# A decoder trunk in fp32: split weights held as three pieces of 2048 columns in place of five of 1024

## The chip, the cores and the metric

The kernel runs on one core of a Trainium2 chip. TensorE multiplies matrices, loading a stationary operand of 128x128 and streaming the other through it; VectorE, ScalarE and GpSimd do the elementwise work; SyncE issues the transfers from the chip's memory (HBM) into the on-chip memory of 128 partitions. The metric is the device time of one execution in microseconds (us), the median of three runs.

## The reference

Two layers on 256 tokens of 1024 channels, all in float32:

```python
a    = rmsnorm(h)
proj = a @ w_in[i]                       # q, k, v, u, c, b: 512 columns each
attn = stick_breaking_attention(qnorm(q), knorm(k), v)      # 8 heads of 64
conv = b * causal_depthwise_conv(c * u)                     # 3 taps
h   += concat(rmsnorm(attn), rmsnorm(conv)) @ w_o[i]
f    = rmsnorm(h)
h   += swiglu(f)                         # layer 0: dense, hidden width 3584
h   += moe_swiglu(f)                     # layer 1: the best 2 of 8 experts of the same width
h   += sigmoid(rmsnorm(h) @ w_g[i]) * (p[i] @ w_p[i])       # the embedding
```

with `swiglu(x) = (silu(x @ w1) * (x @ w3)) @ w2`.

## The kernel before

**Numbers in two parts.** Each fp32 operand is held as a rounded high part and the low remainder, and each product is made of three matmuls: input low by weight high (line 181), input high by weight low (182), high by high (183). So the low part of a weight is wanted one matmul after its high part.

**Weights.** A weight comes in halves of 128 partitions by 2048 columns, 1 MB each. `load` (line 85) gets a slot of the pool `rawp` and issues the transfer. `split` makes the two parts, in slots of the pool `wp`: `wh` by a copy on ScalarE (L94, called a cast below) and `wl` by a subtraction on VectorE (L95). `plan` lists the halves in the order of use, and `parts` cuts each into pieces of `PART` columns, which are the unit of splitting. `loads(upto)` issues transfers up to a part, `prepare(upto)` splits up to a part, and `weights()` hands out the next half and prepares parts so that `ahead[0]` are held, the one in use among them:

```python
NPART = 5        # split parts held
rawp = pool("rawp", 14)
wp = pool("wp", NPART)
prepare(max(i0 + m, i0 + ahead[0] - keep))
```

With `once=True` (in the experts) it also prepares one more part as soon as the second part of a half is taken. A slot of `wp` is free again when the last matmul that reads it is done; a slot of `rawp` when both the cast and the subtraction have read it. The pool `rawp` serves other things too: parts of gathered tokens, `y`, `hout`, the embedding `pp`, q and k.

`pieces[0]` is 2 up to the experts: there each part is split by two casts and two subtractions of half its columns. From the experts on it is 1.

**The order of work.** TensorE's order is the program's throughout. From the routing on, ScalarE's and VectorE's order is the program's too; before that a scheduler places their instructions. So in the experts a cast that waits for a slot of `wp` holds up everything behind it on ScalarE, and a subtraction that waits for its cast everything behind it on VectorE.

**Experts.** `Moe.route` chooses each token's experts and gathers the first two experts' tokens. `Moe.main` goes through eight experts of seven blocks (512 of the 3584 hidden columns). A block has four up halves (12 matmuls of 512 columns each, into `pe`), with the activation `s` on ScalarE (L843) behind the second and the product `m` on VectorE (L846) behind the fourth; then two down halves of the block before (12 matmuls each, into `y`), and between them the four transposes of `m` (L581, `pt`), whose result is again split, `th` on ScalarE (L585) and `tl` on VectorE (L586). After an expert's last down half its `y` is split (L872 and L873), and in the second block of the next expert it is brought back to the tokens' order and added to `hout` (L880 to L882). Within every second expert but the last the next pair's tokens are gathered (L804, `pg`; split at L210 and L211).

**Embedding.** Its two tensors, `p` (512 columns) and `w` (2048 columns), are handed out by two calls of `weights()` at once; 24 matmuls go to `ppp`, and ScalarE copies each result to `pp` (L1048). In layer 1 this goes along with the third block of the last expert, behind its second down half (line 982); in layer 0 it stands ahead of the last block's down halves in the dense feed-forward.

**End.** The last expert's second down half, the return to the tokens' order, and four gate matrices' halves (`gated_embedding`), from where the output is written.

Of the kernel before, what the change touches and what calls it, by code (L numbers as in the profile page):

```python
# [9 lines left out]
F32R = mybir.dt.float32r  # L10
# [6 lines left out]
P = 128  # L17
D = 1024
S = 256
NT = S // P  # L20
KD = D // P
NE = 8
# [3 lines left out]
PART = 1024      # columns of a weight part, split at a time  # L26
NPART = 5        # split parts held
LOADS = (9, 14)  # weight halves whose loads go ahead of the experts, before and after h is split
EMB = 2          # block of the last expert that the last embedding goes along with
EPS = 1e-6  # L30

# columns of the parameter pack
# [6 lines left out]
# columns of the constant pack  # L39
# [5 lines left out]
def trunk(ctx: ExitStack, tc: tile.TileContext, a, out):  # L45
# [4 lines left out]
    rawp = pool("rawp", 14)  # L50
# [8 lines left out]
    # ---- parameters and constants  # L59
# [5 lines left out]
    lt = cst[:, C_LT:C_LT + P]        # [k, m] = k < m  # L65
    iota = cst[:, C_IOTA:C_IOTA + P]
    elow = cst[:, C_E:C_E + 64].rearrange("p (e f) -> p e f", f=NE)   # [e, f] = f < e
    mhalf = const.tile([P, 8], F32, name="mhalf")
    nc.vector.memset(mhalf, -0.5)
    gtr = const.tile([P, P], F32R, name="gtr")     # [k, m] = k > m  # L70
# [9 lines left out]
    # ---- building blocks  # L80
# [17 lines left out]
    def emb(l):  # L98
        """p and w of the embedding, for weights()"""
        return [(a["pT"][l].rearrange("p k s -> p (k s)"), S), (a["w_p"][l], D)]  # L100

    # the weights in the order of their use, in parts of PART columns, split ahead of it
    plan = []
# [29 lines left out]
    def loads(upto):  # L133
        """parts up to that one, loaded"""
        for i in range(len(ready), min(upto, len(parts))):
            (src, n), c = parts[i]
            if i not in raws:
                w = src.shape[-1]
                raw = load(src, w, 2 if i < 4 else 1)
                for j in range(-(-w // PART)):  # L140
                    raws[i + j] = raw[:, j * PART:min(w, (j + 1) * PART)]

    def prepare(upto, eng=nc.vector):
        """parts up to that one, split"""
        loads(upto)
        while len(ready) < min(upto, len(parts)):
            i = len(ready)
            n = parts[i][0][1]
            raw = raws.pop(i)
            ready.append([x.rearrange("p (k n) -> p k n", n=n) for x in split(raw, raw.shape[-1], pieces[0], eng)])  # L150

    def weights(src=None, n=None, once=False, keep=0):
        """function of k that gives block k of the next of the plan, or, where src is given, of that;
        once: each k is used once, in order; keep: parts before it that are still in use"""
        if src is not None:
            width = src.shape[-1]
            raw = load(src, width)
            pw = min(width, PART)
            p = [[x.rearrange("p (k n) -> p k n", n=n) for x in split(raw[:, c:c + pw], pw)]
                 for c in range(0, width, pw)]  # L160
        else:
            (src, n), _ = parts[used[0]]
            i0, m = used[0], -(-src.shape[-1] // PART)
            used[0] += m
            prepare(max(i0 + m, i0 + ahead[0] - keep))
            p = ready[i0:i0 + m]
            ready[i0:i0 + m] = [None] * m
        kp = p[0][0].shape[1]
        seen = set()

        def at(k):
            c = k // kp
            if once and c not in seen:
                seen.add(c)
                if c:
                    prepare(i0 + c + ahead[0])
            return [x[:, k % kp, :] for x in p[c]]
        return at
# [11 lines left out]
    class TokenRstd:  # L190
        """1 / rms of each token of h, [P, NT]: part(n) for each half of the channels, then done()"""
# [21 lines left out]
    def x_tiles(raw=False):  # L213
        """two parts of a transposed input; of two that live at a time, one is raw: in weights' slots"""
        return [rawp.tile([P, KD, S], F32R, tag="raw", name=n) if raw else xp.tile([P, KD, S], F32R, tag=n, name=n)
                for n in ("xh", "xl")]

    class Transposed:
        """gain * h over channels, in two parts, and the token factors; step(k) does channels k, k + 1 of 128"""
# [6 lines left out]
        def step(self, k):  # L226
            # a bank for each channel block, so that two engines read at a time
# [10 lines left out]
        def rest(self):  # L238
            self.step(4)
            self.step(6)  # L240
            if ahead[0] < NPART:
                ahead[0] = NPART
                prepare(used[0] - 2 + NPART)
            self.rs.part(0)
            self.rs.part(1)
            self.rs.done()

    def run(chunks, between=()):
        """chunks in order; between: {i: closures run after chunk i}"""
# [6 lines left out]
    def gemm_tokens(xh, xl, k0s, pss, done, srcs=None, first=False, final=False):  # L256
        """chunks of pss[t] = sum over the next halves [P, 4 k, 512] of x(tokens t).T @ w, from the k's in k0s on;
        first: both token blocks of the first half go along with its k's; final: the last token block goes in two
        parts of the columns, each with its bank and its done()"""
# [46 lines left out]
    # ---- the mixer: attention and short convolution  # L306
    def mixer(l, xt, after):
        """xt: transposed input, whose steps 4 and 6 are still to do where l > 0; after: makes the next one"""
        with tc.tile_pool(name="att", bufs=2) as ap, tc.tile_pool(name="att1", bufs=1) as a1:
            if l == 0:  # L310
# [5 lines left out]
                ready.extend([wp.tile([P, 2, 512], F32R, tag=n, name=n) for n in ("wh", "wl")] for _ in range(2))  # L316
# [5 lines left out]
                for k in range(KD):  # L322
                    scaled_split(xh[:, k, :], xl[:, k, :], xr[:, k, :], par[:, G_MIX + k:G_MIX + k + 1])
                    if k < 4:
                        wh, wl = [x[:, k % 2, :] for x in ready[k // 2]]
# [13 lines left out]
            def v_g():  # L339
                """the values over tokens, and the convolution's input"""  # L340
# [5 lines left out]
            # q, k normalised, of each (j, t)  # L346
            qn = rawp.tile([P, 2 * NT, 512], F32, tag="raw", name="qn")

            def tokens_in():
                # the squares summed over the channels, to tokens  # L350
# [7 lines left out]
            def consts():  # L358
                # of 0 and 1, so the rounding keeps them
# [9 lines left out]
            # q, k: normalised per head over tokens, then transposed; v stays over tokens  # L369
# [31 lines left out]
            # token factors over the free axis, on every partition  # L401
# [136 lines left out]
            # output projection: the two normalised parts, each with its token factor  # L538
# [38 lines left out]
    # ---- feed-forward, dense  # L577
# [11 lines left out]
    def dense(l, xt, fill, nxt):  # L589
        """fill: closures of work for the wait before the last block; nxt(): makes the next transposed input"""  # L590
# [69 lines left out]
    # ---- feed-forward, routed  # L660
    class Parts:
        """h over tokens, in two parts; part(n, t): half n of the channels of token block t"""
# [15 lines left out]
        def block(self, k, t):  # L678
            """channel block k of token block t: low, high"""
            return [self.x[k // 4][:, i, t, k % 4 * P:(k % 4 + 1) * P] for i in (1, 0)]  # L680

    class Route:
        """the two parts of h, and from its logits each expert's tokens and gates"""
# [17 lines left out]
        def half(self, n, t):  # L701
            """channels of half n of token block t, transposed"""
# [17 lines left out]
        def choose(self, mp, rp):  # L720
            self.mp, self.rp = mp, rp
            # rank of each logit; the lower index goes first where two are equal
# [20 lines left out]
            # slot of each token in its expert, and the tokens of each expert  # L743
# [11 lines left out]
        def counts(self):  # L755
            """the largest number of tokens of an expert"""
# [5 lines left out]
        def gates(self):  # L762
            """softmax over the selected logits"""
# [17 lines left out]
    class Gather:  # L781
        """one-hot token to slot matrices of the experts es, and their tokens over channels, in two parts"""
# [10 lines left out]
        def step(self, k, pl=tp, tag="t", apart=False):  # L793
            """channel blocks k, k + 1; apart: each in a bank of its own"""
# [18 lines left out]
        def slots(self, i):  # L813
            """slot to token matrix of expert i, and the token factor of each slot"""
# [12 lines left out]
    def expert_up(ws, b, g, i, rk, fp):  # L827
        """chunks of hidden block b of the slots i of g; rk(): the token factor of each slot"""
# [46 lines left out]
    def combine(hin, hout, y, slT, gcol, n, pl=tp, tag="t", late=None):  # L875
        """hout = hin + gate * (slots back to tokens), half n of the channels; late: takes the sums, to be done then"""
# [12 lines left out]
    class Moe:  # L889
# [7 lines left out]
        def route(self):  # L897
            """choice of the experts, and the first two's tokens"""
# [5 lines left out]
            prepare(n + 1)  # L904
# [6 lines left out]
            loads(n + 2 * LOADS[1])  # L911
# [5 lines left out]
            prepare(n + 2)  # L917
# [5 lines left out]
        def main(self, first, fill):  # L923
            """every expert's first 128 tokens; first: the first two experts' Gather;
            fill: closures of work to do along with the last expert"""
# [57 lines left out]
            # the last block  # L983
# [22 lines left out]
        def over(self):  # L1006
            """every expert's tokens from the 129th on"""
# [24 lines left out]
    # ---- per-layer embedding  # L1032
    def embedding(srcs=None):
        """four closures that make p @ w, of srcs or the next of the plan, and a function that gives
        the tile it goes to"""
# [16 lines left out]
    def gated_embedding(l, pp, xt, p2, nxt=None, src=None):  # L1052
        """h + sigmoid(x @ w) * pp: into h, or, of the last layer, out; nxt(): makes the next transposed input"""
# [29 lines left out]
    with tc.manual_schedule(engines={mybir.EngineType.PE}):  # L1083
# [8 lines left out]
        with tc.tile_pool(name="moe1", bufs=1) as m1, tc.tile_pool(name="moe2", bufs=2) as mp:  # L1092
# [11 lines left out]
            with tc.manual_schedule(engines={mybir.EngineType.Activation, mybir.EngineType.DVE}):  # L1104
                loads(len(ready) + 2 * LOADS[0])
# [4 lines left out]
            # an expert has more than 128 tokens: the others are added, and the end is done again  # L1110
# [9 lines left out]
def _layout(inp):  # L1120
# [4 lines left out]
    def rows(w, kb, nb):  # L1125
        """[..., kb*128*?, N] -> [..., N/nb blocks, K/(kb*128) parts, 128, kb*nb]"""
# [72 lines left out]
```

## Time and profile before

| | |
|---|---|
| median of three runs (1543.73, 1543.99, 1545.69) | 1543.99 us |
| the profiled execution: span from first to last instruction | 1541.0 us |
| TensorE (PE) busy, share of the span, instructions | 1521.9 us, 99%, 7249 |
| TensorE's weight loads (PEld) | 1261.5 us, 82%, 7249 |
| VectorE (DVE) | 1282.6 us, 83%, 1553 |
| ScalarE (ACT) | 1096.0 us, 71%, 1470 |
| GpSimd (POOL) | 92.7 us, 6%, 96 |
| bytes moved, mean rate | 445.84 MB, 289 GB/s |

The span leaves out what lies before the first and behind the last instruction, 3.0 us against the median. A busy engine is one with an instruction under way, waiting for nothing. TensorE's matmuls overlap each other, so that its busy share tells only that it is seldom without one, not at what pace they follow. The experts run from about 540 to 1485 us of the span.

### The profile page before, as it was taken

What the parts mean: (1) busy time and instruction counts of PE and PEld (TensorE: products, weight loads), DVE (VectorE), ACT (ScalarE), POOL (GpSimd) and SP (SyncE); (2) the same over time, 40 slices, a digit from 0 to 9 for tenths busy, and PEclk for the clock granted to TensorE, in tenths of its full rate; (3) what the DMA queues carried; (4) which work ended last, traced back from release to release, by engine and by line L of the source; (5) the groups of instructions that cost most, each with busy time, mean ns of one, the idle gap of its engine ahead of it and who ended that gap; (6) DMA issues with size and microseconds to landing.
All of it is one profiled execution on the core that took longest, in us unless ns stands there. A gap on an engine that the chain in (4) does not pass through costs nothing.

```text
span 1541.0 us, 19945 instructions
## 1 busy us (share of the span) xinstructions
PE 1521.9 (99%) x7249; PEld 1261.5 (82%) x7249; DVE 1282.6 (83%) x1553; ACT 1096.0 (71%) x1470; POOL 92.7 (6%) x96
## 2 busy tenths in 40 slices
PE   7999999999999999999999999999999999999998
PEld 6888888887888788888888888888888888888886
DVE  7886555556788799899899999999999999999895
ACT  5756444446675687878777778787787887877874
POOL 3430000000243000000000000000000000000000
PEclk9999999999999899999999999999999999999999
DMA  9656554343435699897999998999998899999960
GB/s 359 251 197 241 191 186 176 137 162 111 169 148 203 236 379 371 313 349 288 360 372 375 351 361 328 375 408 378 353 360 331 313 362 368 377 343 338 362 259 30
DMA packets 64043, 445.84 MB, mean 289 GB/s; under 512 B 7104, under 2 KB 9024, under 8 KB 10432
## 3 DMA queue, kind: packets, MB, share of 16 engines
q1 hardware_dynamic: 63936, 444.48, 75.8%
q8 instruction: 59, 0.97, 0.2%
q14 instruction: 48, 0.39, 0.1%
HBM read 443.40 MB, written 1.05 MB: 288 GB/s over the span
## 4 chain that ended last, share of the span: by engine, by line
PE 97%; DVE 1%; DMA 0%; ACT 0%; issue 0%; SPq 0%; POOL 0%; DVEq 0%; ACTq 0%
PE pe L181 13%; PE pe L183 13%; PE pe L182 13%; PE y L183 8%; PE y L182 8%; PE y L181 8%; PE p L183 3%; PE p L182 3%; PE p L181 3%; PE pt L581 2%; PE pu L181 2%; PE pu L182 1%; PE pu L183 1%; PE pj L181 1%; PE pj L183 1%; PE pj L182 1%
## 5 line engine op out<-in xcount | busy, mean ns | idle before, releaser
L95 DVE TENSOR_TENSOR wl<-raw,wh 128x1024 fp32r<-128x1024 f32 (+1 forms) x999 | 1017.6, 1058 | 178.8 <-ACT wh L94 167.3
L94 ACT CAST wh<-raw 128x1024 fp32r<-128x1024 f32 (+1 forms) x1000 | 881.4, 913 | 242.8 <-PE pe L183 78.9
L181 PE MATMUL pe<-wh,xl 128*128 128x512 f32 x896 | 350.6, 391 | 0.0
L183 PE MATMUL pe<-wh,xh 128*128 128x512 f32 x896 | 349.2, 390 | 0.0
L182 PE MATMUL pe<-wl,xh 128*128 128x512 f32 x896 | 348.6, 389 | 0.0
L181 PE MATMUL y<-wh,tl 128*128 128x512 f32 x560 | 226.2, 404 | 0.0
L182 PE MATMUL y<-wl,th 128*128 128x512 f32 x560 | 220.8, 394 | 0.5 <-DVE wl L95 0.5
L183 PE MATMUL y<-wh,th 128*128 128x512 f32 x560 | 220.9, 395 | 0.0
L183 PEld LDWEIGHTS pe<-wh,xh 128*128 128x128 f32 x896 | 168.1, 188 | 36.2
L182 PEld LDWEIGHTS pe<-wl,xh 128*128 128x128 f32 x896 | 168.3, 188 | 35.9 <-DVE wl L95 0.4
L181 PEld LDWEIGHTS pe<-wh,xl 128*128 128x128 f32 x896 | 168.2, 188 | 35.1
L183 PEld LDWEIGHTS y<-wh,th 128*128 128x128 f32 x560 | 105.1, 188 | 25.2
L182 PEld LDWEIGHTS y<-wl,th 128*128 128x128 f32 x560 | 105.3, 188 | 22.7 <-DVE wl L95 1.2
L181 PEld LDWEIGHTS y<-wh,tl 128*128 128x128 f32 x560 | 105.3, 188 | 21.6 <-ACT wh L94 0.2
L181 PE MATMUL p<-wh,xl 128*128 128x512 f32 x224 | 87.8, 392 | 0.0
L183 PE MATMUL p<-wh,xh 128*128 128x512 f32 x224 | 87.3, 390 | 0.0
L182 PE MATMUL p<-wl,xh 128*128 128x512 f32 x224 | 87.2, 389 | 0.0
L585 ACT CAST th<-pt 128x512 fp32r<-128x512 f32 x70 | 40.9, 586 | 41.7 <-PE pt L581 41.7
L95 POOL TENSOR_TENSOR wl<-raw,wh 128x1024 fp32r<-128x1024 f32 x1 | 2.4, 2372 | 990.8 <-ACT wh L94 990.8
L181 PE MATMUL pu<-xh,wl 128*128 128x256 f32 x192 | 56.4, 294 | 0.0
L182 PE MATMUL pu<-xl,wh 128*128 128x256 f32 x192 | 54.2, 282 | 0.0
L183 PE MATMUL pu<-xh,wh 128*128 128x256 f32 x192 | 54.2, 282 | 0.0
(203 smaller groups left out, 1565.4 us busy)
## 6 DMA issues: line engine op xcount, KB each, us to landing
raw<-m_w SPq DMA_DIRECT2D x336, 1024.0 KB, 5.7
raw<-d_w SPq DMA_DIRECT2D x42, 1024.0 KB, 4.8
raw<-w_in SPq DMA_DIRECT2D x22, 1024.0 KB, 6.9
raw<-w_o SPq DMA_DIRECT2D x8, 1024.0 KB, 6.7
raw<-w_g SPq DMA_DIRECT2D x8, 1024.0 KB, 4.8
raw<-w_p SPq DMA_DIRECT2D x2, 1024.0 KB, 4.8
raw<-w_in SPq DMA_DIRECT2D x4, 256.0 KB, 4.4
raw<-w_in SPq DMA_DIRECT2D x2, 512.0 KB, 8.8
```

The source lines that it names most:

```text
L94: nc.scalar.copy(wh[:, cs], raw[:, cs])
L95: eng.tensor_sub(wl[:, cs], raw[:, cs], wh[:, cs].bitcast(F32))
L181: nc.tensor.matmul(ps, ll, rh, start=start, stop=False)
L182: nc.tensor.matmul(ps, lh, rl, start=False, stop=False)
L183: nc.tensor.matmul(ps, lh, rh, start=False, stop=stop)
L581: nc.tensor.transpose(pt[:, c * P:(c + 1) * P], m[:, c * P:(c + 1) * P], ident)
L585: nc.scalar.copy(th, pv)
```

## The change

A part becomes a whole half: `PART` is 2048 and `NPART` is 3, so `wp` holds 3 x 2048 columns for each of `wh` and `wl` in place of 5 x 1024. `rawp` has 13 slots in place of 14. What counted two parts to a half now counts one: the loads ahead of the experts (9 halves, then 13 in place of 14), the split of the very first half, the two transfers that it and the second half are loaded in, and the numbers in `prepare`. In the routing one `prepare` of one part goes, and one stays. At the end `ahead[0] = 3` is no longer below `NPART`, so `Transposed.rest` prepares nothing there; the part that GpSimd subtracts is a whole half. Since `pieces[0]` is as it was, pieces are 1024 columns up to the experts (512 before) and 2048 in the experts (1024 before). The embedding's `p` has 512 columns and takes a slot of its own as before, now one of 2048. The rest of the difference is comments, left out here.

```diff
-PART = 1024      # columns of a weight part, split at a time
-NPART = 5        # split parts held
-LOADS = (9, 14)  # weight halves whose loads go ahead of the experts, before and after h is split
+PART = 2048
+NPART = 3
+LOADS = (9, 13)
...
-    rawp = pool("rawp", 14)
+    rawp = pool("rawp", 13)
...
-                raw = load(src, w, 2 if i < 4 else 1)
+                raw = load(src, w, 2 if i < 2 else 1)
...
-                prepare(used[0] - 2 + NPART)
+                prepare(used[0] - 1 + NPART)
...
-                ready.extend([wp.tile([P, 2, 512], F32R, tag=n, name=n) for n in ("wh", "wl")] for _ in range(2))
+                ready.append([wp.tile([P, 4, 512], F32R, tag=n, name=n) for n in ("wh", "wl")])
...
-                        wh, wl = [x[:, k % 2, :] for x in ready[k // 2]]
+                        wh, wl = [x[:, k, :] for x in ready[0]]
...
-            prepare(n + 1)
...
-            loads(n + 2 * LOADS[1])
+            loads(n + LOADS[1])
...
-            prepare(n + 2)
+            prepare(n + 1)
...
-                loads(len(ready) + 2 * LOADS[0])
+                loads(len(ready) + LOADS[0])
```

The order in which ScalarE works around the last expert's embedding, from the activation of the block before it; `pp` are the copies of the embedding, `th` the split of the transposed `m`. Before:

```order
L843 ACTIVATE s<-pe,rslot 128x512
L94 CAST wh<-raw 128x1024 x4
L94 CAST wh<-raw 128x512
L94 CAST wh<-raw 128x1024
L585 CAST th<-pt 128x512
L94 CAST wh<-raw 128x1024 x3
L1048 COPY pp<-ppp 128x512 x4
L94 CAST wh<-raw 128x1024 x6
```

and of the changed kernel:

```order
L843 ACTIVATE s<-pe,rslot 128x512
L94 CAST wh<-raw 128x2048 x2
L94 CAST wh<-raw 128x512
L585 CAST th<-pt 128x512
L94 CAST wh<-raw 128x2048 x2
L1047 COPY pp<-ppp 128x512 x4
L94 CAST wh<-raw 128x2048 x3
```

The cast of 512 columns is `p`. Behind it stood the first part of `w` ahead of `th`; now the whole of `w` stands behind `th`, and one whole half behind it is cast ahead of the copies.

The order in which VectorE works from the end of an expert into the second block of the next; `y` is the split of the expert's result, `hout` the sum over the experts (the last two names are the two token blocks of h). Before:

```order
L95 TENSOR_TENSOR wl<-raw,wh 128x1024 x2
L586 TENSOR_TENSOR tl<-pt,th 128x512
L95 TENSOR_TENSOR wl<-raw,wh 128x1024 x2
L873 TENSOR_TENSOR y<-y 128x512 x2
L95 TENSOR_TENSOR wl<-raw,wh 128x1024 x4
L882 SCALAR_TENSOR_TENSOR hout<-pc,gate,h_97 128x512
L882 SCALAR_TENSOR_TENSOR hout<-pc,gate,h_98 128x512
L95 TENSOR_TENSOR wl<-raw,wh 128x1024 x2
```

The same place of the changed kernel:

```order
L95 TENSOR_TENSOR wl<-raw,wh 128x2048
L586 TENSOR_TENSOR tl<-pt,th 128x512
L95 TENSOR_TENSOR wl<-raw,wh 128x2048
L873 TENSOR_TENSOR y<-y 128x512 x2
L95 TENSOR_TENSOR wl<-raw,wh 128x2048 x2
L882 SCALAR_TENSOR_TENSOR hout<-pc,gate,h_97 128x512
L882 SCALAR_TENSOR_TENSOR hout<-pc,gate,h_98 128x512
L95 TENSOR_TENSOR wl<-raw,wh 128x2048
```

The sequence is the same, with one subtraction of 2048 columns where two of 1024 stood: the two of `y` and the sums `hout` stand behind whole halves as before.

## Rows read from the trace of the kernel before

**Rows 1.** Busy time by stretch: window, length, PE, PEld, DVE, ACT, POOL, clock, DMA, GB/s.
```profile
545.00:1420.00 875.00, 875.00 (x3988) 720.33 (x3988) 813.60 (x790) 695.17 (x764) 0.00 (x0) 1.00 0.92 354
```

**Rows 2.** Waits at the tile raw, 540 to 1500 us: releaser, us, times.
```profile
  DMA raw<-m_w: 2.0, 4
```

**Rows 3.** Groups by form, whole span (columns as in the page's part 5).
```profile
L95 DVE TENSOR_TENSOR wl<-raw,wh 128x1024 fp32r<-128x1024 f32 x678 | 801.0, 1220 | 69.1 <-ACT wh L94 58.9 <-DMA raw<-m_w 1.4
L94 ACT CAST wh<-raw 128x1024 fp32r<-128x1024 f32 x679 | 700.4, 1053 | 120.8 <-PE pe L183 78.6 <-PE y L183 30.5 <-DVE wl L95 2.4
L95 DVE TENSOR_TENSOR wl<-raw,wh 128x512 fp32r<-128x512 f32 x319 | 215.9, 716 | 109.8 <-ACT wh L94 108.4
L94 ACT CAST wh<-raw 128x512 fp32r<-128x512 f32 x319 | 180.4, 618 | 121.8 <-PE p L183 59.5 <-PE y L183 42.2 <-PE po L183 9.3
```

**Rows 4.** Timeline of a regular block: start, length, engine, operation, [idle before, releaser].
```profile
802.93 0.39 PE L181 MATMUL pe<-wh,xl 128*128 128x512 f32 x1
803.13 0.69 ACT L843 ACTIVATE s<-pe,rslot 128x512 f32<-128x512 f32 x1 [0.30 <-PE pe L183]
...
803.72 3.19 ACT L94 CAST wh<-raw 128x1024 fp32r<-128x1024 f32 x3
...
804.79 4.74 DVE L95 TENSOR_TENSOR wl<-raw,wh 128x1024 fp32r<-128x1024 f32 x4 [0.70 <-ACT wh L94]
...
808.37 0.40 PE L181 MATMUL y<-wh,tl 128*128 128x512 f32 x1
...
811.18 0.60 PE L581 MATMUL pt<-cst,m 128*128 128x128 f32 x4
```

**Rows 5.** Timeline of the block after expert 0's end.
```profile
651.61 2.00 ACT L94 CAST wh<-raw 128x1024 fp32r<-128x1024 f32 x2
...
654.97 1.28 DVE L873 TENSOR_TENSOR y<-y 128x512 fp32r<-128x512 f32 x2
...
667.89 0.74 DVE L846 SCALAR_TENSOR_TENSOR m<-pe,rslot,s 128x512 f32<-128x512 f32 x1
...
669.26 0.60 PE L581 MATMUL pt<-cst,m 128*128 128x128 f32 x4
```

**Rows 6.** Timeline of the first expert's first blocks.
```profile
530.17 5.93 ACT L94 CAST wh<-raw 128x1024 fp32r<-128x1024 f32 x6
...
536.59 0.66 PE L581 MATMUL pt<-cst,m 128*128 128x128 f32 x4 [0.22 <-DVE m L846]
```

**Rows 7.** Routing: a stretch (columns of rows 1), then gathering matmuls in the chain.
```profile
516.00:518.00 2.00, 2.00 (x11) 2.00 (x11) 1.84 (x5) 0.92 (x2) 1.58 (x1) 0.50 0.00 0
...
515.44 6.63 PE pg L804 x32
...
734.40 1.91 PE pg L804 x16
```

**Rows 8.** Timeline of the last expert's embedding.
```profile
1425.76 2.00 ACT L94 CAST wh<-raw 128x1024 fp32r<-128x1024 f32 x2
...
1427.87 0.40 PE L181 MATMUL ppp<-wh,wl 128*128 128x512 f32 x1
...
1434.03 5.80 ACT L94 CAST wh<-raw 128x1024 fp32r<-128x1024 f32 x6
...
1435.11 5.76 DVE L95 TENSOR_TENSOR wl<-raw,wh 128x1024 fp32r<-128x1024 f32 x5 [4.73 <-ACT wh L94]
```

**Rows 9.** Timeline of the last down half of layer 0.
```profile
356.85 3.22 ACT L94 CAST wh<-raw 128x512 fp32r<-128x512 f32 x6
...
358.26 0.50 PE L182 MATMUL y<-wl,th 128*128 128x512 f32 x1 [0.23 <-DVE wl L95]
...
359.46 0.50 PE L182 MATMUL y<-wl,th 128*128 128x512 f32 x1 [0.25 <-DVE wl L95]
```

**Rows 10.** Timeline in the attention of layer 1.
```profile
439.89 1.42 POOL L447 TENSOR_TENSOR spl<-sp,sph 128x384 fp32r<-128x384 f32 x1 [0.72 <-ACT sph L445]
...
441.46 0.34 PE L455 MATMUL later<-spl,gtr 128*128 128x384 f32 x1
```

## Prediction

> **What bounds the kernel now.** I read the engines' shares of the page first, then the busy time by stretch, then single groups and the order of time. Across the experts TensorE is busy 875.00 of 875.00 us [rows 1]; its matmuls of 512 columns start every 0.227 us (0.234 in the down projection), and nothing releases them but the matmul before. VectorE is busy 813.60 us of the same stretch. So TensorE sets the end, VectorE is some 7% behind it, and ScalarE has room. The loads are early: in the whole stretch of the experts a cast or subtraction waited 2.0 us in all for a load, four times [rows 2]. A gain can come only from places where TensorE already waits; a loss comes wherever a split weight now arrives later than TensorE wants it.
>
> **The price of a piece.** A subtraction on 1024 columns takes 1.22 us and one on 512 takes 0.72 [rows 3]; four in a row take 4.74 us, one every 1.18 us [rows 4]. From 512 to 1024 the duration grows by 0.50 to 0.53 us, so 2048 columns should take 1.22 + 1.06 = 2.29 us and one should start every 2.25 us. The bounds are 2.05 (the fixed share grows smaller still) and 2.44 (twice 1.22, no saving). A cast takes 1.05 us on 1024 and 0.62 on 512, so 1.91 on 2048 (bounds 1.8 and 2.1). One half (2048 columns) therefore costs VectorE 2.25 us in place of 2.36, some 0.7 us less in a block of six halves. As TensorE waits for none of that, the saving itself is worth nothing.
>
> What changes is how late a weight is. Before, a buffer of 1024 columns was free after six matmuls, its cast began at once, and the subtraction followed 1.05 us later. Now the buffer is free after twelve, and the subtraction starts 1.91 us after the cast does. The slots for split weights grow from five of 1024 to three of 2048, so a half may still be split while the two before it are in use: 2 x 2.72 = 5.44 us for 0.20 + 1.91 + 0.04 + 2.29 + 0.06 = 4.50 us of work, where 0.20 is the time from the start of TensorE's next half to ScalarE's start on what that releases (802.93 to 803.13 [rows 4]), and the small numbers are the gaps between a cast, its subtraction and the matmul behind.
>
> The Trainium skill, Perfetto Trace Analysis, section Optimizing Scalar/DVE Operations, has a rule for each side: larger operations raise throughput if the engine is saturated, and where Scalar or Vector aren't saturated but cause bubbles on other engines, breaking instructions up lets work finish sooner. By the first the 0.7 us of 56 blocks would be 39 us of gain; VectorE was not what TensorE waited for, so the sum takes nothing of it. By the second the change goes the wrong way, which is what the terms below say from rows.
>
> **The regular block** (48 of 56): no loss, with little cover. The up half that starts at 802.93 releases the activation at 803.13 and after it the cast at 803.72 [rows 4]. With the new durations this cast ends at 805.63 and its subtraction at 807.96, and TensorE wants it with its second matmul at 808.37 + 0.23 = 808.60: cover 0.6 us. The next subtraction starts at 807.92 and is followed at 810.17 by the product m (0.74), done at 810.91. The transposes of m stand at 811.18: cover 0.2 us, before 1.0. The term is 0; it becomes a loss from 2.36 us a half on.
>
> **The block after an expert's end** (7 times). VectorE has two more subtractions for y and four sums hout there, and is busy without a break from 654.97 to the product m at 667.89, which ends 0.63 us ahead of the transposes at 669.26 [rows 5]. Now the y subtractions queue behind a whole half, whose cast starts where it started before, at 651.61: 651.61 + 1.91 + 0.04 + 2.25 = 655.8 in place of 654.97. Four halves behind that save some 0.1. So m is done at 669.4 and reaches TensorE 0.2 us late: 7 x 0.2 = 1.4 us, between 0 and 7 x 0.73 = 5.1 (at 2.36 us a half). In the three experts with a new pair gathered VectorE has two more subtractions of 512 in a block, 1.4 us; the fourth up half comes 0.1 late: 0.3 us.
>
> **The first expert.** The casts start only at 530.17, and TensorE already waits for m, until 536.59 [rows 6]. Now 530.17 + 1.91 + 0.04 + 2 x 2.25 + 0.74 + 0.06 = 537.4: 0.8 us later. In the routing the one split left between the choice and the gathered tokens is twice as long, 1.1 us more ahead of eight short subtractions; the gathering matmuls beside them run at a granted clock of 0.50, 1.2 GHz (32 of them in 6.63 us, later 16 in 1.91 [rows 7]), and hide most: 0.3 us. Together 1.1 (0.5 to 2).
>
> **The last expert's embedding, the largest term.** Its two tensors lie between two blocks, p (512 columns) and w (2048), and p fills a slot of 2048. Both are in use at once, so only one half is held ahead. First, w takes the slot of the down half before last. Before, its first part was cast from 1425.76 and was there for the embedding's second matmul at 1427.87 + 0.23 = 1428.10 [rows 8]. Now: 1425.76 + 1.91 + 0.04 + 2.29 + 0.06 = 1430.06, 2.0 us late. Second, behind the embedding TensorE has one half ready and starts on it 24 matmuls later, at 1433.35; the second can only be cast when the embedding's copies are done, at 1434.03. Before, its first part was subtracted from 1435.11 to 1436.33, and TensorE wanted it at 1433.35 + 2.72 + 0.23 = 1436.30. Now 1434.03 + 1.91 + 0.04 + 2.29 + 0.06 = 1438.33: 2.0 us late, 1.9 more than before. Sum 3.8 (3 to 4.5).
>
> **The same place in layer 0.** Pieces there are half a slot: 1024 columns now, 512 before. The last down half is cast from 356.85 and TensorE waits for its subtractions twice already, until 358.26 and 359.46 [rows 9], 0.75 us in all past its pace. With pieces of 1024 the first is there at 356.85 + 1.04 + 0.05 + 1.22 + 0.06 = 359.22, the second 0.5 us behind its want: the two waits grow to about 1.95, less 0.2 that the same pieces save a little later: 1.0 (0.5 to 1.5). Elsewhere in layer 0 a half lasts 5.44 us on TensorE, twice the window, and hides everything.
>
> **Attention and the first matmuls.** The scheduler puts weight pieces between the short steps of the heads. One step ends at 441.31 on GpSimd where TensorE wants it at 441.46 [rows 10]: a piece that is 0.5 us longer ahead of such a step shows. I take 0.5 us a layer, 1.0, between 0 and 4. The first matmuls of the second weight half wait for one piece of 1024 in place of 512: 0.3 (0 to 0.5).
>
> **Raw slots.** One slot less is 2.8 us less lead, and a slot is held some 0.7 us longer. The few waits for loads are small [rows 2], so nothing. The tail takes nothing either: the split given to GpSimd becomes twice as long, but is for the second half of the last gate, 7 us away.
>
> **Sum.** 0.3 + 1.0 + 1.0 + 1.1 + 1.4 + 0.3 + 3.8 = 8.9 us. The profiled span is 1541.0 us, 3.0 below the median of 1544.0, which the change doesn't touch: 1541.0 + 8.9 + 3.0 = 1552.9, say **1553 us**, 0.6% slower.
>
> **Rivals.** (a) *VectorE saves nothing on a wider piece*: a half takes twice 1.22 = 2.44 us. Then the cover of the regular block is gone by 0.17 us, 48 x 0.17 = 8; the seven blocks lose 1.1 each, 8; the rest 9: 1569. Against it: the growth from 512 to 1024 [rows 3]. Values between give 1555 to 1565. (b) *Only the forced places lose*: embedding, first expert, layer 0's end, 5.9 us: 1550. For it: the other terms are each a few tenths, within what I can read off. (c) *Not slower: the pace of the down projection.* Its matmuls start every 0.234 us, those of the up projection every 0.227 (808.37 to 811.18 holds 12 of the one, 802.93 to 808.37 holds 24 of the other [rows 4]). If VectorE's and ScalarE's many short accesses cause this 0.007, fewer of them win up to 1344 x 0.007 = 9 us and cancel the sum: 1544; with (b), 1541. It decides from 4 ns a matmul on. Against it: the up projection runs under the same traffic at the faster pace. A smaller relief of the kind: if TensorE's clock doesn't fall to 1.2 GHz in the routing, 6.63 - 2 x 1.91 = 2.8 us come back; with (b) that is 1547. (d) *The change isn't what it says*: before the experts each half is split in two pieces, so 2048 wide pieces exist only there; this is in the sum.
>
> **How the numbers follow.** Forecast 1553: 0.50. (a) or between, 1557 to 1569: 0.12. (b) 1550: 0.14. No change by (c) or by the clock: 0.16. Faster, (c) with (b): 0.08. A measurement of this kernel tells 0.2% (3 us) from no change. Slower: 0.50 + 0.12 + 0.14 = 0.76; the same 0.16; faster 0.08. The range takes in (b), part of no change, and (a) up to half of it: 1545 to 1563.
>
> **What would show it.** In the trace of the changed kernel: a subtraction on 2048 columns of 2.29 us; TensorE waiting some 2 us twice around the last embedding, for the second matmul of the embedding and of the half after the next; about 0.2 us at the transposes in one block per expert and none in the others; in the first expert 0.8; all else as before. It is wrong if TensorE shows waits in every block (then a piece is dearer), if the embedding's waits aren't there (then a slot is free earlier than I read), if the time sits in attention, or if the matmul pace moves.

## The result

The changed kernel takes 1557.49 us (median of five runs, 1556.61 to 1558.88) against 1544.54 us before: a ratio of 1.0083, 95% interval 1.0073 to 1.0094, 12.95 us slower. The forecast was 1553, with 1545 to 1563 for the range. The profiled execution spans 1556.9 us.

Groups by form of the changed kernel, which answer to [rows 3]:

```profile
L95 DVE TENSOR_TENSOR wl<-raw,wh 128x2048 fp32r<-128x2048 f32 x338 | 768.0, 2289 | 112.7 <-ACT wh L94 110.1 <-DMA raw<-m_w 1.3
L94 ACT CAST wh<-raw 128x2048 fp32r<-128x2048 f32 x339 | 647.3, 1913 | 111.4 <-PE pe L183 86.7 <-PE y L183 17.2 <-DMA raw<-m_w 7.5
...
L95 DVE TENSOR_TENSOR wl<-raw,wh 128x1024 fp32r<-128x1024 f32 x160 | 194.4, 1245 | 115.6 <-ACT wh L94 115.6
...
L94 ACT CAST wh<-raw 128x1024 fp32r<-128x1024 f32 x160 | 161.8, 1048 | 136.0 <-PE p L183 61.8 <-PE y L183 43.3 <-PE po L183 13.2
```

The price of a piece came out as forecast: 2.289 us for a subtraction on 2048 columns (2.29), 1.913 for a cast (1.91). VectorE is busy 1234.0 us in place of 1282.6, and the kernel is slower all the same.

TensorE executes the same 7249 instructions in the same order in every kernel of this study, so that the time from one fixed instruction to another can be set side by side. This table is worked out so from the starts in the traces. "Start" is from the first matmul to the 101st instruction. Counted from 0, the other stretches lie between the instructions 1600, 1760, 2000 and 2570 and between 2630, 2700, 6700 and 6800. From 100 to 1600 all twelve traces take 298.31 us, and behind 6800 they differ by less than 0.4 us. The routing (2570 to 2630) isn't listed, since the granted clock there differs between executions of one kernel: 13.9 and 12.7 us in the two traces of the kernel before, 12.5 to 14.2 in all. The lines below "changed" are the experiments of the next section.

| stretch of TensorE (us) | start | layer 0's end | gates, layer 0 | attention | first expert | experts | last embedding |
|---|---|---|---|---|---|---|---|
| before | 27.13 | 36.29 | 50.86 | 90.46 | 15.20 | 877.93 | 22.66 |
| before, a second trace | 31.35 | 36.31 | 50.85 | 90.46 | 15.21 | 877.94 | 22.64 |
| changed | 30.47 | 37.19 | 51.43 | 90.85 | 15.93 | 883.61 | 26.63 |
| old widths everywhere | 28.94 | 36.31 | 51.15 | 90.46 | 15.21 | 877.94 | 23.20 |
| 1024 in the experts | 29.58 | 37.20 | 51.41 | 90.85 | 15.20 | 877.94 | 23.22 |
| six parts of 1024 | 30.56 | 35.19 | 50.86 | 90.45 | 15.22 | 877.93 | 22.39 |
| raw slots alone | 30.95 | 36.30 | 50.87 | 90.46 | 15.22 | 877.92 | 22.63 |
| p elsewhere | 30.25 | 37.20 | 51.42 | 90.86 | 15.94 | 883.53 | 22.43 |
| cast ahead | 30.38 | 37.19 | 51.42 | 90.85 | 15.93 | 878.01 | 28.21 |
| both | 31.20 | 37.20 | 51.42 | 90.85 | 15.94 | 878.04 | 22.42 |
| both, old widths early | 31.11 | 36.31 | 51.13 | 90.45 | 15.93 | 878.08 | 22.43 |
| and the first expert in 1024 | 31.55 | 36.29 | 51.14 | 90.46 | 15.21 | 878.15 | 22.41 |

From the first and the third line the change costs 0.90 at layer 0's end, 0.57 in the gates, 0.39 in attention, 0.73 in the first expert, 5.68 in the other experts and 3.97 at the last embedding: 12.2 us. The start adds 3.3 between the two traces that were compared first, but not beyond the second trace of the kernel before; it is taken up below.

The two waits of the last expert's embedding, in the timeline (start, length, engine, operation, idle time before):

```profile
1437.50 1.91 ACT L94 CAST wh<-raw 128x2048 fp32r<-128x2048 f32 x1
...
1439.62 0.39 PE L181 MATMUL ppp<-wh,wl 128*128 128x512 f32 x1
...
1441.79 0.50 PE L182 MATMUL ppp<-wl,wh 128*128 128x512 f32 x1 [1.78 <-DVE wl L95]
...
1447.84 5.51 ACT L94 CAST wh<-raw 128x2048 fp32r<-128x2048 f32 x3
...
1449.78 6.69 DVE L95 TENSOR_TENSOR wl<-raw,wh 128x2048 fp32r<-128x2048 f32 x3 [5.73 <-ACT wh L94]
...
1452.12 0.50 PE L182 MATMUL pe<-wl,xh 128*128 128x512 f32 x1 [1.83 <-DVE wl L95]
```

They answer to [rows 8]. `w` is cast at 1437.50, behind `th`, and the embedding's second matmul waits for its subtraction; behind the copies the next half is cast at 1447.84, and the second matmul on it waits again. Against the kernel before, TensorE falls behind by 2.06 and 1.92 us here.

The wait that the prediction had not sized stands where the next pair's tokens are gathered. Timeline of one such block, in the fourth expert; first ScalarE, then VectorE, then TensorE:

```profile
989.47 0.48 ACT L210 ACTIVATE xh<-pg,par 128x256 fp32r<-128x256 f32 x1 [1.76 <-PE pg L804]
991.19 0.84 ACT L210 ACTIVATE xh<-pg,par 128x256 fp32r<-128x256 f32 x2 [1.24 <-DVE xl L211]
992.61 0.48 ACT L210 ACTIVATE xh<-pg,par 128x256 fp32r<-128x256 f32 x1 [0.58 <-DVE xl L211]
992.98 1.90 ACT L94 CAST wh<-raw 128x2048 fp32r<-128x2048 f32 x1
...
990.02 0.74 DVE L846 SCALAR_TENSOR_TENSOR m<-pe,rslot,s 128x512 f32<-128x512 f32 x1
...
993.12 0.48 DVE L211 SCALAR_TENSOR_TENSOR xl<-pg,par,xh 128x256 fp32r<-128x256 f32 x1 [0.54 <-ACT xh L210]
994.91 2.29 DVE L95 TENSOR_TENSOR wl<-raw,wh 128x2048 fp32r<-128x2048 f32 x1 [1.31 <-ACT wh L94]
...
997.25 0.51 PE L182 MATMUL pe<-wl,xh 128*128 128x512 f32 x1 [0.59 <-DVE wl L95]
```

ScalarE's activations `xh` and VectorE's sums `xl` wait for each other in turn, and the cast of the next block's first half stands behind the last `xh` in the program's order. Cast and subtraction then follow one another, and TensorE's second matmul waits for the end of the second. The same place in the kernel before:

```profile
981.63 0.74 DVE L846 SCALAR_TENSOR_TENSOR m<-pe,rslot,s 128x512 f32<-128x512 f32 x1
...
984.59 1.99 ACT L94 CAST wh<-raw 128x1024 fp32r<-128x1024 f32 x2
...
985.65 2.36 DVE L95 TENSOR_TENSOR wl<-raw,wh 128x1024 fp32r<-128x1024 f32 x2 [0.45 <-ACT wh L94]
...
988.57 0.39 PE L182 MATMUL pe<-wl,xh 128*128 128x512 f32 x1
```

There the cast of the first 1024 columns began at 984.59 and their subtraction at 985.65; with 1.22 us for it and 0.06 from a subtraction to its matmul they were ready at 986.93, 1.64 us ahead of that matmul (988.57). A whole half takes 0.86 + 1.07 = 1.93 us more, and VectorE reaches `m`, which the ladder waits for, 0.6 us later (990.02; the 981.63 of before and the 7.77 us by which TensorE is late by then make 989.40): 1.64 - 1.93 - 0.6 = -0.9. TensorE fell back by 0.86 to 0.97 us in each of six such blocks, two per pair, 5.5 us in all.

The smaller waits of TensorE that the change brings, in the order of time: at layer 0's end (to [rows 9]), at the gates behind it, in attention and in the first expert.

```profile
362.43 0.50 PE L182 MATMUL y<-wl,th 128*128 128x512 f32 x1 [0.75 <-DVE wl L95]
...
375.56 0.50 PE L181 MATMUL pgate<-wh,xl 128*128 128x512 f32 x1 [0.72 <-DVE xl L211]
...
431.02 0.63 PE L393 MATMUL pt<-cst,qn 128*128 128x128 f32 x4 [0.21 <-DVE qn L383]
...
539.79 0.50 PE L182 MATMUL pe<-wl,xh 128*128 128x512 f32 x1 [0.58 <-DVE wl L95]
```

The first and the last wait for a subtraction of a weight, the two between for other work of VectorE.

Elsewhere in the experts nothing is late. A regular block and the block after an expert's end of the changed kernel, which answer to [rows 4, 5]:

```profile
817.96 0.74 DVE L846 SCALAR_TENSOR_TENSOR m<-pe,rslot,s 128x512 f32<-128x512 f32 x1
...
819.07 0.60 PE L581 MATMUL pt<-cst,m 128*128 128x128 f32 x4
```

```profile
661.83 1.28 DVE L873 TENSOR_TENSOR y<-y 128x512 fp32r<-128x512 f32 x2
...
674.47 0.74 DVE L846 SCALAR_TENSOR_TENSOR m<-pe,rslot,s 128x512 f32<-128x512 f32 x1
...
675.32 0.61 PE L581 MATMUL pt<-cst,m 128*128 128x128 f32 x4
```

The product is done 0.37 us ahead of the transposes in the first, 0.11 in the second.

### The profile page after: what moved, and what is told of

It reads as the page before. It is cut to its first block, busy times and chain, and to the rows that moved or that the text cites. A ratio compares the mean times of both kernels' runs of the same rounds, so it can differ in the third digit from the quotient of the medians.

```text
span 1556.9 us, 18545 instructions
## 1 busy us (share of the span) xinstructions
PE 1526.9 (98%) x7249; PEld 1261.4 (81%) x7249; DVE 1234.0 (79%) x1055; ACT 1026.6 (66%) x972; POOL 97.3 (6%) x96
## 4 chain that ended last, share of the span: by engine, by line
PE 90%; DVE 4%; ACT 2%; issue 2%; POOL 1%; DMA 1%; SPq 0%; ACTq 0%; DVEq 0%
PE pe L182 12%; PE pe L183 12%; PE pe L181 12%; PE y L183 8%; PE y L182 8%; PE y L181 8%; PE p L183 3%; PE p L182 3%; PE p L181 3%; DVE wl L95 3%; ACT wh L94 2%; PE pt L581 2%; PE pu L181 2%; PE pu L182 1%; PE pu L183 1%
## 5 line engine op out<-in xcount | busy, mean ns | idle before, releaser
L95 DVE TENSOR_TENSOR wl<-raw,wh 128x2048 fp32r<-128x2048 f32 (+1 forms) x501 | 963.8, 1945 | 228.3 <-ACT wh L94 225.7
L94 ACT CAST wh<-raw 128x2048 fp32r<-128x2048 f32 (+1 forms) x502 | 810.4, 1628 | 251.6 <-PE pe L183 87.5
L843 ACT ACTIVATE s<-pe,rslot 128x512 f32<-128x512 f32 x56 | 38.8, 692 | 43.5 <-PE pe L183 43.5
L95 POOL TENSOR_TENSOR wl<-raw,wh 128x2048 fp32r<-128x2048 f32 x1 | 4.6, 4600 | 1000.2 <-ACT wh L94 1000.2
```

The source lines that it names most:

```text
L94: nc.scalar.copy(wh[:, cs], raw[:, cs])
L95: eng.tensor_sub(wl[:, cs], raw[:, cs], wh[:, cs].bitcast(F32))
L843: nc.scalar.activation(st["s"], st[0], AF.Silu, scale=rk())
```

## The experiments

**Theories.** L: what is late is the longer cast and subtraction that stand ahead of the first matmuls of a half, at the few places where a half is split just in time. S: what is late is the slot, which is free only after twelve matmuls, however the half is split. R: the raw slot that was taken away.

**Old widths in the new slots.** The first run has 512 columns up to the experts and 1024 in them, as before; the second only the 1024 in the experts.

```diff
-    pieces = [2]
+    pieces = [4]
...
-            pieces[0] = 1
+            pieces[0] = 2
```

> The changed kernel with its three slots of 2048 columns, but every cast and subtraction as wide as in the kernel before (512 columns up to the experts, 1024 in them). Theory L (what is late is the longer cast and subtraction ahead of the first matmul of a half): the six waits of 0.75 to 0.97 us behind the gathering of a pair, the 0.73 us of the first expert, 3.5 of the 4.15 us at the last expert's embedding and the 1.9 us at layer 0's end and in attention go, so some 12 us of the 13: 1545 to 1547 us. Theory S (a slot of 2048 is free only after twelve matmuls, however the half is split): the waits stay, 1555 us or more.

> The changed kernel, with casts and subtractions of 1024 columns in the experts alone; up to the experts its own (1024). Theory L: 5.5 (gathering) + 0.7 (first expert) + 3.5 (embedding) = 9.7 us less than the changed kernel, 1547.8 us, and the difference to the run with all the old widths, about 2 us, is the price of the wider pieces in layer 0 and attention. Theory S: as the changed kernel within 2 us.

Measured: 1548.14 us with the old widths everywhere (ratio to the kernel before 1.0022, 1.0012 to 1.0031), 1548.73 with 1024 in the experts (1.0024, 1.0014 to 1.0034). Some 9 us of the 13 are gone in both. In the table the experts and the first expert are back at the numbers of before, with slots of 2048 that are free no earlier; 0.6 us stay at the embedding. S falls, L stands. The first run is 1.1 us above the upper end of what was expected. The difference of the two medians is smaller than the 2 us that were expected. The trace shows why: the early widths give back 0.9 + 0.3 + 0.4 us, but a new wait of 1.26 us stands in the first attention:

```profile
26.97 2.58 DVE L95 TENSOR_TENSOR wl<-raw,wh 128x512 fp32r<-128x512 f32 x4
29.48 0.68 DVE L383 TENSOR_TENSOR qn<-pj,r 128x512 f32<-128x512 f32 x1
...
30.25 0.63 PE L393 MATMUL pt<-cst,qn 128*128 128x128 f32 x4 [1.26 <-issue]
```

That is the timeline of the run with the old widths. The page names no releaser, but `qn` is what the transposes read: the scheduler puts four subtractions ahead of it, where the kernel before has two and no wait:

```profile
26.61 1.29 DVE L95 TENSOR_TENSOR wl<-raw,wh 128x512 fp32r<-128x512 f32 x2
27.82 0.69 DVE L383 TENSOR_TENSOR qn<-pj,r 128x512 f32<-128x512 f32 x1
...
28.60 0.63 PE L393 MATMUL pt<-cst,qn 128*128 128x128 f32 x4
```

With more columns held there may be more small pieces ready to be put there; no run tests that.

**The capacity in the old grain, and the raw slot alone.**

```diff
-NPART = 5
+NPART = 6
...
-LOADS = (9, 14)
+LOADS = (9, 13)
...
-    rawp = pool("rawp", 14)
+    rawp = pool("rawp", 13)
```

The second of the two runs is without the first pair of lines.

> The kernel before with six parts of 1024 in place of five and 13 raw slots in place of 14: the memory of the changed kernel, split in its old grain. Theory L and theory S both: no wait of the changed kernel is there, 1544 us, within 1.5 us of the kernel before. A rival, that the 13 raw slots or the larger hold cost something by themselves, gives several us more, 1548 to 1557.

> The kernel before with 13 raw slots in place of 14 and nothing else of the change. The prediction's step: nothing, 1544.5 us within 1. The rival, that a shorter lead of the loads makes the casts wait: several us more, with waits for loads that grow from the 2.0 us of before.

Measured: 1545.15 us (1.0001, 0.9992 to 1.0011) and 1545.01 (1.0000, 0.9991 to 1.0009). R falls: a raw slot less is worth nothing. The same memory in parts of 1024 is worth nothing either, though it takes the waits at layer 0's end away (35.19 for 36.29): a wait of 1.26 us at the same transposes of `qn` as above stands against it.

**The embedding alone.** `p` gets a raw slot for its two split parts, and is not counted among the three:

```diff
-        wh = wp.tile([P, w], F32R, tag="wh", name="wh")
-        wl = wp.tile([P, w], F32R, tag="wl", name="wl")
+        if own[0] and w <= 512:
+            t = rawp.tile([P, 2, w], F32R, tag="raw", name="pw")
+            wh, wl = t[:, 0], t[:, 1]
+        else:
+            wh = wp.tile([P, w], F32R, tag="wh", name="wh")
+            wl = wp.tile([P, w], F32R, tag="wl", name="wl")
...
-            prepare(max(i0 + m, i0 + ahead[0] - keep))
+            end = i0 + ahead[0] - keep
+            if own[0] and any(x[0].shape[-1] <= 512 for x, _ in parts[i0:end + keep]):
+                end += 1
+                keep = 0
+            prepare(max(i0 + m, end))
```

> The changed kernel with one thing altered: in the experts the embedding's p (512 columns) takes a raw slot in place of one of the three slots for split weights, so that w is split one half earlier and two halves are held behind it. Theory: the two waits of 2.10 and 2.05 us at the last expert's embedding come from p's slot alone and both go: 4.1 us less than the changed kernel, 1553.4 us; the six waits behind the gathering stay. Rival: the waits are the length of a cast and a subtraction wherever they queue, and one of the two, or a later half, still waits: 1555.5 us or more.

Measured: 1553.38 us (1.0059, 1.0045 to 1.0073), 4.1 less than the changed kernel, as expected. Its timeline on ScalarE:

```profile
1431.58 0.62 ACT L99 CAST pw<-raw 128x512 fp32r<-128x512 f32 x1
1432.47 1.92 ACT L99 CAST wh<-raw 128x2048 fp32r<-128x2048 f32 x1 [0.28 <-PE pe L192]
1435.71 0.59 ACT L594 CAST th<-pt 128x512 fp32r<-128x512 f32 x1 [1.32 <-PE pt L590]
1436.19 1.92 ACT L99 CAST wh<-raw 128x2048 fp32r<-128x2048 f32 x1
1438.52 1.92 ACT L99 CAST wh<-raw 128x2048 fp32r<-128x2048 f32 x1 [0.40 <-PE y L192]
1440.34 0.58 ACT L1056 COPY pp<-ppp 128x512 f32<-128x512 f32 x1
```

`w` is cast ahead of `th`, and two more halves ahead of the copies; TensorE has no wait there (22.43 in the table). So one tensor of 512 columns in a slot of 2048 cost 4 us together with the wide casts and subtractions; with 1024 columns at a time in the same slots 0.6 us of it was left.

**The gathering alone.** The cast of the next half is taken out of `prepare` and put ahead of the two gathering steps of a block; the subtraction stays where it was:

```diff
+    def cast_ahead():
+        i = len(ready)
+        loads(i + 1)
+        raw = raws[i]
+        w = raw.shape[-1]
+        wh = wp.tile([P, w], F32R, tag="wh", name="wh")
+        wl = wp.tile([P, w], F32R, tag="wl", name="wl")
+        nc.scalar.copy(wh, raw)
+        casted[i] = (wh, wl)
...
                         elif b > 4:
+                            cast_ahead()
```

> The changed kernel with one thing altered: in the two blocks of a pair in which tokens are gathered, the cast of the next expert block's first half stands ahead of the four activations xh on ScalarE, whose slot is free by then; its subtraction stays behind the four sums xl. Theory: these six waits (0.75 to 0.97 us, 5.5 in all) come from that cast queueing behind the ladder xh, xl, xh: it ends some 2.4 us earlier, the subtraction follows the last xl at once and is in time by some 0.3 us: 1552.0 us. Rival: VectorE is what is late (it splits two tensors more there), and the subtraction stays late: 1555 us or more; a worse one, the ladder itself moves by the cast and the transposes of m wait for its bank: as the changed kernel or above.

Measured: 1552.79 us (1.0052, 1.0038 to 1.0066), 4.7 less than the changed kernel. All six waits are gone (878.01 in the table). The block shown above, ScalarE first:

```profile
986.64 1.91 ACT L152 CAST wh<-raw 128x2048 fp32r<-128x2048 f32 x1 [0.80 <-PE pe L200]
988.46 0.47 ACT L227 ACTIVATE xh<-pg,par 128x256 fp32r<-128x256 f32 x1
...
990.90 0.47 ACT L227 ACTIVATE xh<-pg,par 128x256 fp32r<-128x256 f32 x1 [0.58 <-DVE xl L228]
...
991.41 0.48 DVE L228 SCALAR_TENSOR_TENSOR xl<-pg,par,xh 128x256 fp32r<-128x256 f32 x1 [0.54 <-ACT xh L227]
991.81 2.28 DVE L164 TENSOR_TENSOR wl<-raw,wh 128x2048 fp32r<-128x2048 f32 x1
```

The cast takes the time in which ScalarE waited for the first gathered tokens, and the subtraction follows the last `xl` without the 1.31 us of waiting in the changed kernel. The median fell by 0.8 us less than the sum. In the profiled execution the granted clock fell behind the wait that it still has at the embedding, and the stretch is 1.6 us longer than in the changed kernel (28.21 for 26.63); whether the other four executions had the same is not known. They were 1.5 to 2.3 us shorter, at a mean granted clock of 0.995 where the profiled one had 0.992.

**Both, and what is left.** Three kernels: both edits together; then with the old 512 columns up to the experts; then with 1024 in the first two blocks of the first expert as well (and, as the width is set ahead of it, in the one split of the routing). Of the lines below the first two belong to the second and third kernel, the others to the third alone.

```diff
-    pieces = [2]
+    pieces = [4]
...
-            pieces[0] = 1
+            pieces[0] = 2
...
+                    if (e, b) == (0, 2):
+                        pieces[0] = 1
```

> Both alterations together, pieces as in the changed kernel. If the two sums add, 1557.5 - 4.1 - 5.5 = 1547.9 us; the rest over the kernel before is the first expert (0.7) and layer 0 and attention (1.9).

> Both alterations, and up to the experts casts and subtractions of 512 columns as in the kernel before; 2048 in the experts. Theory: 1.9 us less than with both alone, 1546 us: what is left over the kernel before is the first expert and the start. VectorE's saving of some 40 us of work is not seen in the time, since TensorE doesn't wait for it; a rival is that it is, and the time falls below the kernel before.

> The last kernel (both alterations, old pieces up to the experts) with casts and subtractions of 1024 columns also in the first two blocks of the first expert; 2048 from there on. Theory: the last wait of the ledger that the change brings, 0.63 to 0.73 us at the first expert's second matmul, goes: 1546.5 us, and the trace from the start of the experts on stands no later against the kernel before than ahead of them. Rival: that wait is the routing's, not the piece's, and stays.

Measured: 1548.51 us (1.0024, 1.0015 to 1.0033), 1547.24 (1.0015, 1.0006 to 1.0024) and 1547.44 (1.0016, 1.0007 to 1.0025). The two large terms add up. The last wait, in the first expert, goes in the trace (15.21 for 15.93), but the median doesn't show it: that 0.7 us is less than the runs differ by. The last kernel stands 2.65 us above the 1544.79 of the kernel before, of which its trace accounts for 1.6; the rest is taken up behind the next run. What remains in the last kernel's trace is 0.3 in the gates and, within the start, the wait of 1.3 us at `qn`. VectorE is busy 1249.1 us in the kernel with the old widths early, 33.5 less than before, and none of it appears in the time: no kernel here has a median below that of the one before.

**The start.** The kernel before once more, for a second trace.

> The kernel before, unchanged, for a second trace of its start. If the fall of the granted clock behind TensorE's idle stretch at 14 to 17 us is a matter of the single execution and not of the change, this trace may show it too (3 us at most by some 24 us); if the trace of before is typical, this one shows none, and the 3 us of the changed kernel's start belong to the change.

One run, 1546.01 us, its span 1544.0. Busy time by stretch (the columns of [rows 1]), of the kernel before in its first trace, in its second, and of the changed kernel:

```profile
14.00:18.00 4.00, 2.19 (x12) 1.60 (x11) 4.00 (x9) 2.49 (x5) 0.86 (x2) 1.00 1.01 422
18.00:25.00 7.00, 7.00 (x32) 5.78 (x31) 5.88 (x15) 4.27 (x9) 0.92 (x2) 1.00 1.03 419
```

```profile
14.00:18.00 4.00, 0.80 (x4) 0.36 (x3) 4.00 (x9) 2.71 (x7) 1.51 (x3) 0.96 1.02 425
18.00:25.00 7.00, 7.00 (x20) 5.64 (x20) 5.16 (x12) 2.25 (x5) 0.71 (x1) 0.54 1.02 415
```

```profile
18.00:25.00 7.00, 7.00 (x21) 5.70 (x22) 5.05 (x9) 2.25 (x3) 0.72 (x1) 0.60 1.02 415
```

In its second trace the kernel before has 20 matmuls between 18 and 25 us where the first had 32, at a granted clock of 0.54: most of that stretch at 1.2 GHz, after TensorE had stood idle for most of 14 to 18 us (busy 0.80 of 4.00 us, in the first trace 2.19). So the kernel before has the longer start too, its first trace had the shorter one, and the 3.3 us between the traces that were compared first aren't the price of the change.

Whether the change makes the clock fall more often is another question, which single traces can't answer. The mean granted clock over the whole span is known for each execution. It was 0.993 or less in 27 of 68 executions of kernels with three slots of 2048, and in none of 67 of the kernel before or of 22 of its two variants (six parts, 13 raw slots). Within one kernel the executions at 0.993 are 1 to 2 us longer: with the old widths everywhere 1548.99 us on the mean of five, against 1546.80 of three at 0.995. At the same 0.994 the last kernel is 1.5 us above the kernel before (1546.65 and 1545.14 on the mean), about what its trace accounts for. So the lower clock can be what the medians have beyond the sums of the traces, up to about 1 us; no run here alters the clock alone, and the cause stays open.

## Why the prediction was right, point by point

- **The price of a piece**: 2.289 and 1.913 us, as forecast (1.22 + 1.06 is 2.28, which changes nothing). Rival (a) falls.
- **Regular block**, cover 0.2 us forecast, 0.37 measured, no loss: right.
- **Block after an expert's end**, 1.4 us forecast, none measured. The subtractions of `y` came where they were put, but the four halves and sums behind them saved 0.28 us (11.36 in place of 11.64 from `y`'s end to `m`) and not 0.1, and so `m` is 0.11 early and not 0.2 late. The 0.1 didn't follow from the prediction's own price: four halves at 2.25 in place of 2.36 us save 0.4, by which the term would have been nothing.
- **Experts with a new pair**, 0.3 forecast, 5.5 measured: the term that was mis-sized. It counted the two more subtractions of `h` on VectorE, and not the ladder of `xh` and `xl` in the two blocks behind, at whose end the next half's cast and subtraction stand one after the other. Moving that cast alone gave the 5.5 back in the trace.
- **First expert and routing**, 1.1 forecast. The first expert's 0.73 us is the size forecast (0.8), but stands at a matmul that wants a subtraction, one half ahead of the transposes that were named; 1024 columns take it away. The routing can't be told from the clock's own changes there.
- **The last embedding**, 3.8 forecast (its two parts, 1.96 and 1.9, add to 3.9), 3.97 measured, at the two matmuls named, and gone with `p` out of the three slots: right in place and size, and in the cause: the slot that `p` fills and the length of a cast and a subtraction together.
- **Layer 0's end**, 1.0 forecast, 0.90 measured. Not forecast was 0.57 in the gates behind it, where the gate's input waits for VectorE.
- **Attention**, 1.0 forecast, 0.39 measured; **start**, 0.3, not to be told from the clock's own 3 us.
- **Raw slots**: nothing, by the run with that alone.
- **From span to median**: the prediction took the 3.0 us between the first trace's span and the median for time outside the span. The runs of the changed kernel have 1.8 to 2.0 us there, the second trace of the kernel before has 2.0 (1546.01 less 1544.0); the other 1.0 or so goes with the first trace's short start. The forecast isn't moved by it, since its sum stands on the median, but the first comparison of the two traces is.
- **The rivals**: (b), which leaves only the forced places, was too small by the gathering; (c), a relief of the matmul pace, is not seen: where the experts have no wait, with 2048 columns, they take 878.08 us against 877.93. The measured 1557.49 lies in the band that was given to (a) "or between", 1557 to 1569, but not by its cause.
- **The signs of being wrong**: waits in every block, no waits at the embedding, time in attention and another matmul pace were named, and none came. But "all else as before" didn't hold: six waits stand behind the gathering, and a small one in the gates.

The Trainium skill, Perfetto Trace Analysis, section Optimizing Scalar/DVE Operations, says that breaking up instructions may let work finish sooner where Scalar and Vector aren't saturated and cause bubbles elsewhere. The runs agree: the old widths in the new slots gave back some 9 us of the 13.

So the sum of 8.9 stands against 12.2 in the trace and 12.95 in the medians. The gathering alone was short by 5.2, and the gates by 0.6; the terms that didn't come or came smaller, above all the 1.4 behind an expert's end and 0.6 in attention, made up for part of it. That the time lies within the range is therefore in part luck: its upper part was there for a dearer piece. The direction, the largest forecast term and the way in which a late weight costs time were right for the reason given.

## What to carry to other kernels

Wider instructions on an engine that nobody waits for bought nothing here; they lengthen the time from a free slot to a usable tile, and this costs where a tile is made just in time. To find these places, list every operation that stands ahead of a tile's preparation in its engines' order (copies, splits of other data, ladders between two engines), not only the added work on the busiest engine. And a small tensor that takes a slot sized for the large ones costs a whole slot of lead: a place of its own took that cost away.

## What the runs showed of the hardware that was not expected

The granted clock differs between executions of one kernel: behind TensorE's idle stretch at the start it was 1.00 and 0.54 over 18 to 25 us in two traces of the kernel before, whose spans are 1541.0 and 1544.0 us. And in one trace it fell behind a shorter wait: in the run with the cast ahead, after the wait of nearly 2 us in the last embedding, it was 0.50 where the changed kernel had kept 1.00 behind the same wait (1441.80 to 1445.00).

```profile
1436.60:1440.00 3.40, 3.40 (x10) 2.63 (x9) 1.81 (x1) 0.59 (x1) 0.00 (x0) 0.50 0.86 301
```

```profile
1441.80:1445.00 3.20, 3.20 (x14) 2.65 (x15) 2.25 (x1) 0.95 (x2) 0.00 (x0) 1.00 0.82 289
```

The first is of the run with the cast ahead, the second of the changed kernel: ten matmuls in 3.4 us against fourteen in 3.2. A comparison of two single traces therefore has to be made stretch by stretch, with the clock's column beside it.
